# Operands normalised before their split, sums read from PSUM by ScalarE and by the convolution, weights in half blocks, and another order of the units

## The chip, the cores and the metric

The kernel runs on one core of a Trainium2 chip. Its metric is the device time of one execution in microseconds (us). Every number here is of float32 data; the large products are made of pieces that TensorE takes as `float32r`.

## The reference, cut to what matters

One inference step of a two-layer decoder trunk, for 512 prompt tokens and 8 sample tokens (520 columns in all) of 1024 features:

```python
xn = rmsnorm(x, g_mix)                       # over the 1024 features of a token
u_a, v_a, q, k, v, gate_a, gate_b = split(xn @ w_in)     # 512, 512, 3 x 768, 2 x 1024 columns
a_out = chunk_spatial_gate(gelu(u_a), rmsnorm(gelu(v_a), g_v), w_s, b_s)
q, k = rope(rmsnorm(q)), rope(rmsnorm(k))    # 12 heads of 64: three pairs (window, dilation)
b_out = windowed attention of each pair, the pairs merged by their softmax denominators
merged = sigmoid(gate_a) * (a_out @ w_a_proj) + sigmoid(gate_b) * (b_out @ w_b_proj)
x = x + merged @ w_o
up = rmsnorm(x, g_ffn) @ w_up                # 5632 columns
c = conv_b + sum(conv_w[j] * up shifted by 2 - j tokens for j in 0, 1, 2)
x = x + (silu(c_gate) * c_val) @ w_down      # 2816 inputs
```

Outputs are the new x of both token groups, new key and value rows, the last two up-projected rows and the samples' v rows.

## The kernel before, in words

Everything lies with features on the 128 partitions and the 520 tokens as columns. An output **unit** is 128 output features. Weights and activations are each split into a high part and a low part (what is left over), and a product is three matmuls: high x high, high x low, low x high. A matmul takes 128 inputs and 260 of the 520 columns, so a unit of eight input tiles is 48 matmuls, summed in an accumulator of two PSUM banks. `dense` (L263) issues a unit through `products` (L243, its matmul L252). `dense_first` (L383) does the first three units of layer 0 input by input, and `dense(xs, 2)` the first two of the other stages that follow a norm.

The weights of a unit are one load on SP's queue (`load_raw`, up to 512 KB) and one split (`split`, L187): ScalarE copies the high part (L193), VectorE subtracts (L194). Loads run three units ahead, splits two.

`Norm` does not normalise its operands: it splits x times the gain (L291, L292), sums the squares beside that, and a task (`rms`, lane "n") makes 1/rms per token, spread over all partitions. Every unit that reads such operands is multiplied by it as it leaves PSUM, on VectorE: L870 and L876 for q, k, v; L894 for u and v of the gate (`gelu2`, which goes on on GpSimd and ScalarE); L1051 for the gates, whose tanh follows on ScalarE (L1052); L1097 for the FFN. There `up_conv` then applies three taps to the copy in SBUF: one on ScalarE (L1100), two on VectorE (L1102).

The order of units in a layer is the list `units`: q, k, v of pair 2, four v units, pair 1, four u units, pair 0, then gate a and w_a in turn (eight of each), three gates b, then w_b and the other gates b in turn (b5, b6, b7 without a gate between them), eight units of w_o, and the FFN: 22 pairs of up units, the down work in three pieces of 8, 7 and 7 inputs, each eight units in a row after the first up pair of the next piece.

Attention, spatial gate, samples' attention, history and output rows are generators in lanes. `pump` weaves their stages between the matmuls by an estimate of time, `finish` forces lanes to their end. They use two PSUM banks for transposes (`tps`) and one score tile of two banks (`sc_tile`). The samples' attention multiplies cached values by weights on GpSimd (L834) and adds them on VectorE (L842, L844). From this program a planner that simulates the timeline makes each engine's fixed order; operations inside `urgent()` get a higher priority. Each engine then takes its instructions in that order.

## Time and profile before

| | |
|---|---|
| timed runs, median of 3 | 1584.09 us (1583.84 to 1584.78) |
| profiled execution, first to last instruction | 1582.3 us |
| TensorE busy | 1550.8 us (98%) |
| weight loads of TensorE busy | 1522.5 us (96%) |
| VectorE, ScalarE, GpSimd busy | 934.2, 648.2, 515.6 us |
| matmuls | 12985 recorded |

The span of the profiled execution is the only time that the page gives of it; it goes from the first to the last instruction, and the timed runs lie 1.8 us above it. A group of instructions is named by its line, engine, operation and tiles; "idle before" is what the engine waited in front of them, and the arrow names what released it. A window is a stretch of the span in us from its start. A few matmul records can be missing.

### The profile page before, as it was taken

The numbers are of one execution on the slowest core, as the hardware profiler recorded it, in microseconds if no ns is written. First come the engines' busy times: TensorE is split into PE (matmuls) and PEld (weight loads), VectorE is DVE, ScalarE is ACT, GpSimd is POOL, SyncE is SP. The second block draws the span as 40 slices with busy tenths as digits, with TensorE's granted clock in tenths as the row PEclk, the third lists the DMA queues.
The fourth block names the chain that finished last, engine by engine and source line by source line (L and its number), as shares of the span: only waits on it lengthen the run. The fifth ranks groups of instructions, "written<-read, shape, count | busy, mean of one in ns | idle before, by whom it ended". The sixth has DMA issues, their size and how long they took to land. (4 is left out here: it accounts for less than half of the span.)

```text
span 1582.3 us, 31439 instructions
## 1 busy us (share of the span) xinstructions
PE 1550.8 (98%) x12985; PEld 1522.5 (96%) x12985; DVE 934.2 (59%) x1344; ACT 648.2 (41%) x1155; POOL 515.6 (33%) x677
## 2 busy tenths in 40 slices
PE   8999999899999999999999999998999999999998
PEld 7989899899999999999999999998999999999998
DVE  6576856855466456556437585757655663564652
ACT  5454536334444234334435544552334441442342
POOL 3645453623222012213228272636222220220130
PEclk9999999999999999999999999999999999999999
DMA  7443333424233333332344332433332333323322
GB/s 211 132 115 112 95 107 102 152 78 131 84 94 94 94 94 86 88 95 85 108 113 126 111 125 79 120 113 113 99 115 82 93 94 94 94 84 104 92 73 70
DMA packets 294845, 164.24 MB, mean 104 GB/s; under 512 B 14143, under 2 KB 288335, under 8 KB 294687
## 3 DMA queue, kind: packets, MB, share of 16 engines
q1 hardware_dynamic: 294703, 162.24, 35.0%
q8 instruction: 102, 1.67, 0.4%
q14 instruction: 40, 0.33, 0.1%
HBM read 154.66 MB, written 10.36 MB: 104 GB/s over the span
## 5 line engine op out<-in xcount | busy, mean ns | idle before, releaser
L252 PE MATMUL acc<-t,whi 128*128 128x260 f32 x7776 | 1276.4, 285 | 11.1 <-DVE t L1051 8.7
L252 PEld LDWEIGHTS acc<-t,whi 128*128 128x128 f32 x7776 | 1070.7, 189 | 18.4 <-issue 11.6
L252 PE MATMUL acc<-t,wlo 128*128 128x260 f32 x3888 | 785.5, 284 | 0.0
L252 PEld LDWEIGHTS acc<-t,wlo 128*128 128x128 f32 x3888 | 600.4, 189 | 1.4 <-issue 0.7
L193 ACT CAST whi<-raw 128x1024 fp32r<-128x1024 f32 (+3 forms) x268 | 260.5, 973 | 457.4 <-PE acc L252 287.5
L194 DVE TENSOR_TENSOR wlo<-raw,whi 128x1024 fp32r<-128x1024 f32 (+3 forms) x268 | 323.0, 1206 | 40.3 <-ACT whi L193 22.9
L1097 DVE TENSOR_TENSOR t<-acc,t 128x520 f32<-128x520 f32 x88 | 61.5, 699 | 158.2 <-PE acc L252 158.2
L1098 POOL COPY ut<-t 128x10 f32<-128x10 f32 x88 | 30.9, 351 | 364.5 <-DVE t L1097 361.1
L1102 DVE SCALAR_TENSOR_TENSOR t<-t,cwc,t 128x511 f32<-128x511 f32 (+1 forms) x176 | 131.6, 749 | 4.9 <-ACT t L1100 1.8
L1131 DVE TENSOR_TENSOR x<-acc,x 128x520 f32<-128x520 f32 x48 | 33.5, 700 | 148.2 <-PE acc L252 148.2
L1124 POOL TENSOR_TENSOR t<-t,t 128x520 fp32r<-128x520 f32 x44 | 58.9, 1339 | 127.1 <-ACT t L1123 127.1
L300 POOL TENSOR_TENSOR t<-t,t 128x520 f32<-128x520 f32 x25 | 44.0, 1762 | 110.1 <-ACT t L299 107.5
L1100 ACT ACTIVATE t<-t,vcol,cwc 128x520 f32<-128x520 f32 x88 | 72.5, 824 | 5.8 <-DVE t L1097 5.5
L1123 ACT CAST t<-t 128x520 fp32r<-128x520 f32 x44 | 27.6, 627 | 115.2 <-DVE t L1121 115.2
L506 POOL TENSOR_TENSOR t<-t,t 128x128 f32<-128x128 f32 x96 | 56.7, 619 | 18.8 <-DVE ss L499 18.2
L1105 POOL TENSOR_TENSOR t<-t,hc 128x8 f32<-128x8 f32 x88 | 45.4, 515 | 49.7 <-ACT t L1100 49.7
L1120 ACT ACTIVATE t<-t 128x520 f32<-128x520 f32 x44 | 28.1, 639 | 81.1 <-DVE t L1102 81.1
L1075 POOL TENSOR_TENSOR t<-t,t 128x520 f32<-128x520 f32 x16 | 23.6, 1482 | 80.5 <-DVE t L1074 80.5
L653 ACT ACTIVATE t<-t,stat 128x128 f32<-128x128 f32 (+1 forms) x96 | 40.1, 420 | 22.9 <-DVE stat L650 22.7
L136 POOL TENSOR_TENSOR rr<-ss,mhalf 128x8 f32<-128x8 f32 (+1 forms) x30 | 49.0, 1632 | 0.0
L1051 DVE TENSOR_TENSOR t<-acc,t 128x520 f32<-128x520 f32 x32 | 22.2, 695 | 43.7 <-PE acc L252 43.7
L775 POOL TENSOR_TENSOR t<-t,t 128x512 f32<-128x512 f32 x24 | 35.1, 1473 | 30.3 <-DMA t<-in_cache_kv_w_dram 25.4
(195 smaller groups left out, 1172.2 us busy)
## 6 DMA issues: line engine op xcount, KB each, us to landing
raw<-in_w_up_dram SPq DMA_DIRECT2D x88, 512.0 KB
raw<-in_w_in_dram SPq DMA_DIRECT2D x84, 512.0 KB
raw<-in_w_down_dram SPq DMA_DIRECT2D x32, 448.0 KB
t<-in_cache_kv_w_dram SPq DMA_DIRECT2D x48, 256.0 KB
raw<-in_w_o_dram SPq DMA_DIRECT2D x16, 512.0 KB
raw<-in_w_down_dram SPq DMA_DIRECT2D x16, 512.0 KB
raw<-in_w_a_proj_dram SPq DMA_DIRECT2D x16, 256.0 KB
out_dram<-t SPq DMA_DIRECT2D x15, 256.0 KB
```

The source lines that it names most:

```text
L136: pool.tensor_tensor(out, in_, mhalf[: in_.shape[0], :n], op=ALU.pow)
L193: act.copy(hi[:, :nk], r)
L194: eng.tensor_tensor(lo[:, :nk], r, hi[:, :nk].bitcast(F32), op=ALU.subtract)
L252: mm = pe.matmul(acc[:, h, :H2], w[:, k], m[:, h * H2 : h * H2 + H2], start=(k == 0 and i == 0), stop=(k == last and i == 2),)
L300: eng.tensor_tensor(self.ssum[i], self.ssum[i], sq, op=ALU.add)
L506: pool.tensor_tensor(s4[:, i, :, s : s + 32], q4[:, i, :, d : d + 32], ts_[:n, i : i + 1, s : s + 32].to_broadcast([n, 4, 32]), op=ALU.mult,)
L653: act.activation(S[:, hp], S[:, hp], AF.Exp, bias=nmx[:, i : i + 1], accum_out=stat[:, 4 + i : 5 + i])
L1097: dve.tensor_tensor(v2(up), acc, rb, op=ALU.mult)
L1100: act.activation(cv, up, AF.Identity, scale=cwc[:, 2, i : i + 1], bias=vcol[:, 32 + i : 33 + i])
L1102: dve.scalar_tensor_tensor(cv[:, s:TP], up[:, : TP - s], cwc[:, j, i : i + 1], cv[:, s:TP], op0=ALU.mult, op1=ALU.add)
L1105: pool.tensor_tensor(cv[:, TP:], cv[:, TP:], hc[:, :, m], op=ALU.add)
L1124: pool.tensor_tensor(lo, cg, hi.bitcast(F32), op=ALU.subtract)
```

## The change

- Weights are loaded and split in blocks of at most four input tiles (half a unit), with a ring of six split blocks and nine raw ones.
- Accumulators are five single banks, transposes and scores share three banks; a score takes two of those three.
- `dense` takes any number of units at once and hands each one's two banks to a function `unit`, inside `urgent()`. The first two units after a norm, of w_o and of the last down piece (three in layer 0's start) are taken input by input.
- After 1/rms is there, a second task (`operands`, lane "x") multiplies x by gain and 1/rms and splits the product again; `dense2` uses these operands, so nothing has to be multiplied on the way out of PSUM. It serves pairs 1 and 0, u, v, all gates, and the up units from the fourth on (`NSTD = 3`).
- Their sums are read from PSUM by ScalarE (q, k, v, u, v: copies; gates: tanh), and in the FFN by the three taps (`psum_conv`).
- Gates come in pairs: g g, g g a a, g g a a, g g a a, a a; then for b the order `mix`. The down work is four pieces of 7, 5, 5 and 5 inputs, of which three are spread between later up pairs.
- `SEVEN` names unit pairs that would be computed as seven products of half operands; it is empty.

```diff
-NSLOT = 66
+NSLOT = 61
+RING = 6
+RAWS = 9
+NSTD = 3
+SEVEN = ()
...
     def acc_tile():
-        return ps.tile([128, 2, 512], F32, tag="acc", name=nm("acc"))
+        return ps.tile([128, 512], F32, tag="acc", bufs=5, name=nm("acc"))[:, :H2]
     def tps():
-        return ps.tile([128, 512], F32, tag="tp", name=nm("tp"))
+        return ps.tile([128, 512], F32, tag="tp", bufs=3, name=nm("tp"))
...
+    pieces = ((0, 7), (7, 12), (12, 17), (17, 22))
+    for i in range(22):
+        ffn.append(("up", i))
+        for g, i0, ns in ((0, 8, (2, 2, 2, 2)), (1, 13, (2, 2, 2, 2)), (2, 18, (1, 1, 2, 4))):
+            if 0 <= i - i0 < 4:
+                ffn.extend(("down", g, sum(ns[: i - i0]) + j) for j in range(ns[i - i0]))
+    mix = ("g0", "g1", "b0", "g2", "b1", "b2", "g3", "b3", "b4", "b5", "b6", "b7")
...
     def feed():
+        while st["split"] < len(blocks) and (st["split"] < RING or st["split"] - RING in st["used"]):
+            split()
+        while st["raw"] < len(loads) and st["raw"] < st["taken"] + RAWS - 4:
+            load_raw()
...
+    def dense(xs, unit, lows_last=False):
+        banks = [[acc_tile(), acc_tile() if j < 2 else tps()[:, :H2]] for j in range(len(cs))]
+        def taken(j):
+            finish("n")
+            with urgent():
+                unit(j, *banks[j])
+        for k0, k1 in ks:
+            for j, c in enumerate(cs):
+                held[j, k0] = block(g, (k0, c))
+            last = k1 == nk and not lows_last
+            for js in [[j] for j in range(len(cs))] if last else [range(len(cs))]:
+                for k in range(k0, k1):
+                    for j in js:
+                        hi, lo = held[j, k0]
+                        triple((hi[:, k - k0], lo[:, k - k0]), xs[k], banks[j], k == 0, k == nk - 1, ...)
+                if last:
+                    taken(js[0])
...
+    def dense2(norm, unit, done):
+        finish("n", "x")
+        if groups[st["g"]][0] == "u":
+            for j in range(2):
+                dense(norm.xn, lambda _, *accs, j=j: unit(j, *accs))
+            return
...
+        def operands(self):
+            while any(tasks["n"]):
+                yield -1.0
+            for s in range(7 if self.seven else 5):
+                with urgent():
+                    for m in (s, s + 4) if s < 4 else ():
+                        xm = tmp()
+                        dve.scalar_tensor_tensor(xm, x[:, m], vcol[...], self.rbc, op0=ALU.mult, op1=ALU.mult)
+                        high(m, xm)
+                    if 0 <= s - 1 < 4:
+                        for m, i in ((k, (1, 0)), (k + 4, (2, 3))):
+                            xn[m] = low(m)
+                yield -0.7
...
-            sc = sc_tile()
+            sc = [tps(), tps()]
...
+        def copied(g, accs):
+            for h, acc in enumerate(accs):
+                act.copy(v2(g)[:, h], acc)
...
-        def gate(g):
-            acc = dense(xs)
-            with urgent():
-                dve.tensor_tensor(v2(g), acc, rb, op=ALU.mult)
-            act.activation(g, g, AF.Tanh, scale=0.5)
+            def unit(j, *accs):
+                g[j] = tmp()
+                for h, acc in enumerate(accs):
+                    act.activation(v2(g[j])[:, h], acc, AF.Tanh, scale=0.5)
...
+        m1, gb, mgs = [], [], []
+        for j in range(5):
+            if j < 4:
+                m1.extend(gates())
+            if j == 1:
+                finish("v")
+            for i in (2 * j - 2, 2 * j - 1) if j else ():
+                gated(m1[i], As)
+        for g, j in mix:
+            if g == "g":
+                gb.extend(gates())
+                continue
+            if j == 0:
+                finish("a", "s")
+            gated(gb[j], Bx)
...
+        def psum_conv(m, z0, z1):
+            for h, z in enumerate((z0, z1)):
+                act.activation(v2(cv)[:, h], z, AF.Identity, scale=cwc[...], bias=vcol[...])
+            act.copy(ut[:, :, m], z1[:, 510 - H2 :])
+            for j, s in ((1, 1), (0, 2)):
+                for z, c0, c1 in ((z0, s, H2), (z0, H2, H2 + s), (z1, H2 + s, TP)):
+                    src = z[:, c0 - s : c1 - s] if z is z0 else z[:, c0 - s - H2 : c1 - s - H2]
+                    dve.scalar_tensor_tensor(cv[:, c0:c1], src, cwc[...], cv[:, c0:c1], op0=ALU.mult, op1=ALU.add)
```

## Rows read from the trace of the kernel before

**Rows 1.** The page's first section: busy time of each engine, share of the span, instructions.
```profile
PE 1550.8 (98%) x12985; PEld 1522.5 (96%) x12985; DVE 934.2 (59%) x1344; ACT 648.2 (41%) x1155; POOL 515.6 (33%) x677
```

**Rows 2.** Waits of TensorE over the span: waited for, us in total, times, longest us.
```profile
PE acc L252 <- DVE t L1051: 8.7, 4, 4.0
...
PE tp L368 <- DMA t<-in_x_prompt_dram: 3.0, 2, 1.8
PE sc L630 <- DVE t L644: 2.7, 5, 1.2
PE tp L612 <- DVE t L521: 2.6, 3, 1.5
PE acc L252 <- DVE t L1074: 2.3, 2, 1.2
```

**Rows 3.** Stretches: length, busy us (instructions) by engine, granted clock, DMA share, GB/s.
```profile
0.00:20.00 20.00, 12.97 (x77) 11.78 (x78) 11.71 (x20) 11.26 (x17) 4.41 (x7) 1.00 0.98 263
33.00:53.00 20.00, 20.00 (x168) 20.00 (x169) 8.11 (x10) 9.17 (x16) 4.75 (x3) 1.00 0.70 200
60.00:100.00 40.00, 35.70 (x300) 33.80 (x300) 32.79 (x54) 20.55 (x48) 32.70 (x36) 1.00 0.42 124
...
300.00:400.00 100.00, 94.28 (x773) 93.72 (x772) 61.97 (x76) 34.68 (x54) 31.20 (x26) 0.98 0.36 106
430.00:760.00 330.00, 330.00 (x2762) 330.00 (x2761) 187.20 (x225) 120.79 (x145) 65.03 (x106) 1.00 0.32 92
```

**Rows 4.** Groups by line and shape over the span: count, busy us, mean ns; idle before.
```profile
L194 DVE TENSOR_TENSOR wlo<-raw,whi 128x1024 fp32r<-128x1024 f32 x204 | 269.7, 1322 | 38.6 <-ACT whi L193 22.5 <-issue 1.3 <-PE acc L252 0.8
L193 ACT CAST whi<-raw 128x1024 fp32r<-128x1024 f32 x204 | 214.2, 1050 | 336.0 <-PE acc L252 209.2 <-issue 115.1 <-DMA raw<-in_w_in_dram 8.2
L1100 ACT ACTIVATE t<-t,vcol,cwc 128x520 f32<-128x520 f32 x88 | 72.5, 824 | 5.8 <-DVE t L1097 5.5
...
L1102 DVE SCALAR_TENSOR_TENSOR t<-t,cwc,t 128x511 f32<-128x511 f32 x88 | 65.8, 748 | 1.8 <-ACT t L1100 1.8
L1097 DVE TENSOR_TENSOR t<-acc,t 128x520 f32<-128x520 f32 x88 | 61.5, 699 | 158.2 <-PE acc L252 158.2
...
L292 DVE SCALAR_TENSOR_TENSOR t<-x,vcol,t 128x520 fp32r<-128x520 f32 x32 | 25.8, 817 | 0.0
...
L335 DVE TENSOR_TENSOR t<-t,t 128x520 fp32r<-128x520 f32 x24 | 17.4, 733 | 7.7 <-ACT t L334 7.7
...
L644 DVE TENSOR_TENSOR t<-sc,cst 128x256 f32<-128x256 f32 x36 | 13.5, 411 | 0.0
...
L194 DVE TENSOR_TENSOR wlo<-raw,whi 128x512 fp32r<-128x512 f32 x16 | 11.4, 715 | 0.5 <-ACT whi L193 0.5
...
L193 ACT CAST whi<-raw 128x512 fp32r<-128x512 f32 x16 | 9.9, 618 | 11.5 <-issue 9.6 <-PE acc L252 1.7
...
L581 ACT COPY t<-tp 128x256 f32<-128x256 f32 x24 | 8.9, 369 | 9.5 <-PE tp L580 9.3
```

**Rows 5.** Timeline of VectorE around the first long wait: start us, us, engine line.
```profile
300.44 2.54 DVE L842 TENSOR_TENSOR t<-t,t 128x512 f32<-128x512 f32 x2
303.08 1.09 DVE L844 TENSOR_TENSOR t<-t,t 128x256 f32<-128x256 f32 x1
304.09 0.69 DVE L1051 TENSOR_TENSOR t<-acc,t 128x520 f32<-128x520 f32 x1
```

**Rows 6.** Timeline of ScalarE in the same stretch, idle us before it in brackets.
```profile
304.81 0.64 ACT L1052 ACTIVATE t<-t 128x520 f32<-128x520 f32 x1 [5.90 <-DVE t L1051]
```

**Rows 7.** Timeline of VectorE in the run of b units of layer 0.
```profile
364.46 2.35 DVE L194 TENSOR_TENSOR wlo<-raw,whi 128x1024 fp32r<-128x1024 f32 x1 [0.20 <-ACT whi L193]
366.73 0.68 DVE L1074 SCALAR_TENSOR_TENSOR t<-t,acc 128x520 f32<-128x520 f32 x1
```

**Rows 8.** Timeline of VectorE: first and last evacuation of layer 0's first six units.
```profile
33.57 0.69 DVE L876 TENSOR_TENSOR t<-acc,t 128x520 f32<-128x520 f32 x1
...
52.44 0.70 DVE L876 TENSOR_TENSOR t<-acc,t 128x520 f32<-128x520 f32 x1 [3.65 <-PE acc L252]
```

More of the change, by code (lines that the diff above doesn't have):

```diff
@@ new lines, in step_kernel @@
+        for j in range(2, 8):
+            one(a["w_o"][l], 0, 8, j * 128)
+        for op, i, *m in ffn:
+            if op == "down":
+                k0, k1 = pieces[i]
+                one(a["w_down"][l], k0, k1 - k0, m[0] * 128)
+            elif i == 0:
+                one(a["w_up"][l], 0, 8, 0, DFF)
+            elif i < NSTD:
+                one(a["w_up"][l], 0, 8, i * 128)
+                one(a["w_up"][l], 0, 8, DFF + i * 128)
+            else:
+                two(("up", i), a["w_up"][l], DFF + i * 128, i * 128)
@@ L178, in urgent, with load_raw @@
+    raws, splits, parts4 = [], {}, {}
+    st = {"raw": 0, "taken": 0, "split": 0, "used": set(), "g": 0, "now": 0.0, "last": -9.0,
+          "pin": False}
+    at = {b: i for i, b in enumerate(blocks)}
     def urgent():
         return tc.high_priority(URGENT)
-    def load_raw(u):
-        w, k0, nk, c0 = units[u]
-        r = wp.tile([128, 8, 128], F32, tag="raw", bufs=4, name=nm("raw"))
+    def load_raw():
+        w, k0, nk, c0 = loads[st["raw"]]
+        st["raw"] += 1
+        r = wp.tile([128, 4, 128], F32, tag="raw", bufs=RAWS, name=nm("raw"))
@@ L184, in load_raw, with next_raw @@
         dma(r[:, :nk], w[k0 * 128 : (k0 + nk) * 128, c0 : c0 + 128].rearrange("(k p) m -> p k m", p=128))
[L185 to L191 removed]
+        raws.append(r[:, :nk])
+    def next_raw():
+        if not raws:
+            load_raw()
+        st["taken"] += 1
+        return raws.pop(0)
@@ L263, in dense, with triple @@
-    def dense(xs, n=1):
-        us = []
-        for _ in range(n):
-            feed()
-            us.append((*splits.pop(st["u"]), acc_tile()))
-            st["u"] += 1
-        nk = len(xs)
-        assert all(u[2] == nk for u in us)
-        for k in range(nk):
-            products(us, xs, k, (0, 1, 2), nk - 1)
-        accs = [u[3][:, :, :H2] for u in us]
-        return accs if n > 1 else accs[0]
+    def triple(w, x, bank, start, stop, which=(0, 1, 2)):
+        pump()
+        st["now"] += 0.12 * len(which) * len(bank)
+        for i in which:
+            wi, xi = ((w[0], x[0]), (w[0], x[1]), (w[1], x[0]))[i]
+            for h, b in enumerate(bank):
+                mm = pe.matmul(
+                    b,
+                    wi,
+                    xi[:, h * H2 : h * H2 + H2],
+                    start=start and i == 0,
+                    stop=stop and i == 2,
+                )
+                if st["pin"]:
+                    tc.keep_in_program_order(mm)
+                    st["pin"] = False
@@ new lines, in qkv_units @@
+            n = 3 if l == 0 else 2
+            first = [0]
+            def unit(j, *accs):
+                g = tmp()
+                normed(g, accs)
+                have(first[0] + j, g)
+            dense(xs, unit, l == 0)
+            if l == 0:
+                t = tps()
+                pe.transpose(t[:, :104], vrow[:104], ident[:104, :104])
+                act.copy(vcol[:, 16:], t[:, :104])
+            for i in range(n, 6):
+                first[0] = i
+                dense(xs, unit)
@@ L1054, in step_kernel, with gates, unit, done @@
-        m1 = []
-        for j in range(8):
-            g = tmp()
-            gate(g)
-            if j == 0:
-                finish("v")
-            acc = dense(As)
-            with urgent():
-                dve.scalar_tensor_tensor(v2(g), v2(g), 1.0, acc, op0=ALU.add, op1=ALU.mult)
-            m1.append(g)
-        add("v", history())
-        gb = [tmp() for _ in range(8)]
-        for j in range(NGB):
-            gate(gb[j])
-        finish("a", "s")
-        mgs = []
-        for j in range(8):
+        def gates():
+            g = {}
+            def unit(j, *accs):
+                g[j] = tmp()
+                for h, acc in enumerate(accs):
+                    act.activation(v2(g[j])[:, h], acc, AF.Tanh, scale=0.5)
+            def done(j, t):
+                g[j] = t
+                act.activation(t, t, AF.Tanh, scale=0.5)
+            dense2(norm, unit, done)
+            return [g[0], g[1]]
```

475 lines of the change are left out of this document (302 added, 173 removed).

## The prediction, made before the change was run

> **What bounds the kernel now.** I read the page's first section first: TensorE is busy 1550.8 of 1582.3 us [rows 1]. So at most 31.5 us of the span can be won without taking matmuls away, and no matmul is taken away: `SEVEN` is empty, so `dense2` always takes its first branch, two calls of `dense`, and a unit of eight inputs is still 8 x 3 x 2 = 48 matmuls of 260 columns. The seven-product code of the diff never runs. The table of stretches then says what a matmul costs: in the FFN 2762 fill 330.00 us without a gap, 0.1195 us each [rows 3]. A unit of eight inputs lasts 48 x 0.1195 = 5.7 us, one of four 2.9, of two 1.4; a down unit of seven inputs 5.0, of five 3.6.
>
> Where the 31.5 us lie is in the same table: 7.0 in the first 20 us, 4.3 in 60:100, 5.7 in 300:400, none in the FFN [rows 3]. The view of waits names them: 8.7 us for accumulators that a gate's evacuation (L1051) had not freed, four times, 4.0 at the longest; 2.3 for accumulators behind L1074, the b units' evacuation; 3.0 for the first inputs; 2.7 for the score tile; 2.6 for turned q and k [rows 2]. The second layer repeats the first.
>
> What the longest wait is made of is read from VectorE's timeline. The gate's evacuation starts at 304.09, because VectorE's queue is in order and holds the adds L842 and L844 of the samples' attention ahead of it: from 300.44 on they run one behind the other, 2.54 and 1.09 us [rows 5]. Meanwhile ScalarE stood idle for 5.90 us [rows 6].
>
> **The change part by part.** All terms are of the span of the profiled execution, 1582.3; the median of the timed runs, 1584.09, is 1.8 above it, and I add that 1.8 at the end.
>
> *Gates evacuated by ScalarE, in pairs.* The multiply by 1/rms (32 on VectorE, like the 0.699 of L1097) goes; Tanh is taken from the two PSUM banks, 2 x about 0.37 (the 256-column PSUM copy of L581) [rows 4]. In the two long stalls ScalarE was free [rows 6], so these evacuations no longer stand behind L842: of 8.7 us all could go. But the w_a evacuations stay on VectorE, and the new order puts four of them (a4 to a7) in a row just where the samples' adds run. A block of 4 us against a slack of one unit (2.9 us, since with five banks unit n+2 needs the first bank of unit n) leaves 1.1 us per layer. Bounds -8.7 and 0; I take -6.5.
>
> *b units.* Before, b5 to b7 run without a gate between them and cost 2.3 us in two layers: a weight split of 2.35 us stood ahead of an evacuation [rows 7]. Now five run in a row, 5 x 1.4 = 7.2 us, in which VectorE has 10 half evacuations of 0.41 (L644, 256 columns out of PSUM), five half splits of 0.715 and some of the L335 of 0.733 [rows 4]: 4.1 + 3.6 + 1.5 = 9.2 us of work. The backlog of 2.0 less a slack of 1.4 is 0.6 us by undisturbed durations; with the splits as slow as the row of 2.35 against 1.322 shows [rows 4, 7] it is 2 to 3. Bounds -2.3 (five banks absorb it) and +4; I take +1.5 for both layers.
>
> *Tokens normalised ahead.* Four norms get a second set of operands: 8 multiplies (0.817, as L292) and 8 subtracts (0.733, as L335) on VectorE, 12.4 us, and 8 copies on ScalarE of about 0.64, as a plain 520-column pass has it (5.1 us) [rows 4, 6]. In the FFN six units with the old operands (34 us) cover them, in layer 1 too. In layer 0 it is tight: 1/rms is there when the first evacuation starts, 33.57, and the sixth unit ends where its evacuation starts, 52.44 [rows 8]. In 33:53 VectorE has 8.1 us of work now [rows 3]; 12.4 more make 20.5 of 20, while the first unit on the new operands needs the fourth input only 2.2 us later and is taken input by input. Bounds 0 and +4 (12.4 of work against the 11.9 free, and a queue that is sometimes wrongly ordered); I take +0.5. There are 61 tile slots for 66, with 16 more tiles alive while both sets are; that can hold back stages beside the path, whose last date, `finish("a", "s")` ahead of b0, lies one gate (5.7 us) later than now: nothing.
>
> *First units input by input, weights in halves.* Each half is loaded and split by itself: ScalarE 2 x 0.618 for 1.050, VectorE 2 x 0.715 for 1.322 [rows 4], 0.2 and 0.1 us more per unit of 5.7, beside TensorE. The prefetch is no shorter (six half blocks split, five more loaded). Weight loads stand in SP's queue between the x loads at the start; half of each is 256 KB less three times, at 263 GB/s [rows 3] one microsecond each, and 3.0 us were waited for x there [rows 2]. VectorE limits what follows, so I take -1, bounds -2 and +1. The pairs at the start of w_o and of the last down piece win nothing: TensorE does not wait there now.
>
> *PSUM.* Before: two accumulators of two banks, one score tile of two, two for transposes. Now: five single accumulator banks and three for transposes and scores; a score takes two of these three. TensorE takes its instructions in order, so a transpose placed too early waits. Now the score tile costs 2.7 us in five waits; the longest sum of a transpose's waits, 2.6 us, is for its data, not for a bank [rows 2]. If score waits double and transposes wait 2.6 more, +5.3; if VectorE, relieved of the evacuations of q, k, v and of gelu (40 x 0.699 [rows 4]), is earlier with the scores, -2.7. I take +1.
> The Trainium skill (Perfetto Trace Analysis, Optimization Strategy) has a rule that speaks against this edit: the same gap repeating on the engine that should be saturated can mean that there is not enough SBUF or PSUM for the next tile. By it the score gaps should grow with the loss of a bank, +5.3 or more; by the rows alone, five waits among many scores, I stay at +1. It is the first rival below.
>
> *FFN.* Per up unit VectorE's 0.699 + 2 x 0.748 = 2.2 becomes four taps of 260 columns at 0.41 and two of one or two columns (at most 0.41, I take 0.2): 2.0. ScalarE's 0.824 becomes two halves of about 0.37 + 0.18 (the 0.18 is what L1100 with its scale and bias columns takes over a plain 520-column pass of 0.64) [rows 4, 6]. A unit's first bank is free 2 x 0.55 + 0.2 + 0.41 + 0.41 + 0.2 = 2.3 us after its last matmul, and is needed after one more unit: 5.7 us, or 3.6 where a down unit of five inputs follows. That holds with 1.3 us to spare, so 0; the cover gone (ScalarE and VectorE each behind another half split, +1.3) it would be some tenths at each of about 14 such places, +5. VectorE is at 187 of 330 us here [rows 3]. The down work in four pieces instead of three is 16 more evacuations in all, off the path.
>
> *Tail.* The last evacuation is two halves, 2 x 0.41 for 0.699: +0.1, nothing.
>
> Sum: -6.5 + 1.5 + 0.5 - 1 + 1 = -4.5. 1582.3 - 4.5 = 1577.8, and with the 1.8 a median of 1579.6 us.
>
> **The rivals.**
> 1. *Three banks are too few* (slower). In each attention block two of three banks are held until both masks are added; every transpose of the other three blocks in flight, of the merges and of the spatial gate goes through the third. For it: in 60:100 VectorE is at 32.8 and GpSimd at 32.7 of 40 us [rows 3], so banks are freed late. Against: only 2.7 us for 24 scores so far [rows 2]. If each of the 24 scores costs 0.6 us, about the mean of the five waits (2.7/5 = 0.54), that is 14 less the 2.7 there now: +11.3 in place of my +1, 1589.9. From 0.34 us a score on ((5.5 + 2.7) / 24) the gain is eaten up.
> 2. *The stall moves to the w_a units* (no change). The block of adds in VectorE's queue [rows 5] stays, and four short units in a row meet it with less slack than a gate of 5.7 us. Then the -6.5 is about -2 and the rest +2: 1584.1. Against it: a fifth bank.
> 3. *VectorE's relief reaches the attention too.* 72 evacuations of 0.7 us leave its queue (32 + 40). All of the gates' 8.7 goes and half of the waits on L521 and L644 (2.65 of 5.3 [rows 2]), the b run costs what it cost: -8.7 - 2.65 - 1 + 0.5 = -11.85, 1572.2. Against it: GpSimd, on which many of VectorE's attention steps wait, is not relieved of anything in 60:100.
>
> **How the numbers follow.** The forecast gets 0.53, the first rival 0.20, the second 0.15, the third 0.12. A measurement tells 0.2% (3.2 us) from nothing: faster is below 1580.9. The forecast's own range is 1575 to 1584, since its terms' bounds rarely add up; three quarters of it are faster, 0.40, a fifth no change. With the third rival, faster is 0.52; no change 0.11 + 0.13 = 0.24; slower 0.20 from the first rival and 0.04 from the edges, 0.24. The range of eight in ten runs from the third rival's time to the first's, 1572 to 1590.
>
> **What would show it.** Right: TensorE's busy time stays at 1550 to 1551 and the FFN's matmuls at 0.1195 us; no wait of an accumulator for a gate; about 1 us per layer of waits on the w_a evacuation; some waits behind L1074's successor in the run of five b units; at 52 us a gap under 2. Wrong: score and transpose waits beyond 8 us in all (the first rival), accumulators that wait for the conv in the FFN, a change of the matmul's pace, or a start that loses more than it wins.

## The result, and the profile of the changed kernel

The changed kernel takes 1622.91 us (median of 4 runs, 1620.63 to 1625.82) where the kernel before, beside it, took 1584.43: 1.0241 times the time, interval 1.0226 to 1.0255. The forecast was 1579.6 with a range up to 1590, so the sign was wrong too. The profiled execution spans 1618.5 us, 36.2 more than before.

The page's line of busy times, which answers to [rows 1] (engine, busy us, share, instructions):

```profile
PE 1565.9 (97%) x12985; PEld 1535.5 (95%) x12985; DVE 974.9 (60%) x1984; ACT 750.5 (46%) x1719; POOL 449.0 (28%) x601
```

TensorE executes the same 12985 matmuls, but is busy for 15.1 us more and idle for 52.6 instead of 31.5. The waits of TensorE, which answer to [rows 2] (waited for, us in total, times, longest):

```profile
PE acc L339 <- DVE t L1123: 12.2, 8, 2.3
PE acc L339 <- DVE t L1307: 11.7, 2, 6.0
PE acc L339 <- ACT t L1060: 4.9, 4, 1.4
...
PE tp L810 <- DVE t L719: 3.6, 3, 1.3
PE tp L476 <- POOL rc L137: 2.1, 1, 2.1
PE tp L1177 <- POOL t L1154: 2.0, 1, 2.0
PE tp L587 <- DMA t<-in_x_prompt_dram: 2.0, 3, 0.7
PE tp L866 <- ACT t L868: 1.7, 2, 1.5
PE tp L828 <- ACT t L813: 1.6, 2, 0.8
```

An evacuation is the instruction that reads a finished sum out of its accumulator and so frees the bank. L1123 is that of the units that still use the old operands (`normed`, VectorE), L1307 the one of w_a (`gated`, VectorE), L1060 the copy of q, k, v (ScalarE). No line is a gate's tanh. The stretches of [rows 3] (length; busy us by engine in the order PE, PEld, DVE, ACT, POOL; granted clock; DMA share; GB/s), and three more, of the stall at w_a, layer 0's first up units and layer 1's start:

```profile
0.00:20.00 20.00, 13.98 (x85) 12.53 (x86) 12.28 (x21) 8.91 (x15) 5.76 (x10) 1.00 0.80 217
33.00:53.00 20.00, 16.31 (x118) 14.85 (x118) 15.95 (x27) 9.81 (x18) 5.33 (x4) 0.91 0.46 125
60.00:100.00 40.00, 37.72 (x306) 35.90 (x306) 31.43 (x55) 24.01 (x59) 29.47 (x35) 1.00 0.43 124
300.00:400.00 100.00, 93.87 (x766) 93.46 (x765) 58.65 (x95) 34.72 (x73) 30.35 (x26) 0.97 0.33 97
312.00:318.00 6.00, 4.03 (x18) 4.03 (x19) 5.82 (x12) 0.00 (x0) 0.26 (x1) 0.50 0.31 91
427.00:468.00 41.00, 37.24 (x307) 36.59 (x307) 30.39 (x54) 21.51 (x35) 9.10 (x13) 1.00 0.28 79
800.00:900.00 100.00, 94.72 (x741) 92.12 (x740) 66.25 (x117) 57.44 (x125) 42.51 (x45) 0.95 0.42 118
```

33:53 holds 118 matmuls for 168 before. From 312 to 318 the clock stands at 0.50, its lower level, 1.2 GHz. The trace's clock records show such stretches of 3.4 us or twice that six times before the tail, 27 us in all (at 38.7, 311.7, 830.6, 840.8, 885.2 and 1107.0 us, each during or shortly after a stall of TensorE); the kernel before has two, 6.8 us in all. 18 matmuls take 4.03 us there, where 18 of 0.1195 us are 2.15. If a matmul takes twice as long in all of these stretches, they cost up to half their length, 13.6 us against 3.4; in 4.5 of the 27 us TensorE stood anyway, which leaves some 8 us more than before. That is about half of the 15.1 us by which TensorE's busy time rose with the same work. Of the rest 3 us lie in layer 0's first stage; what makes them was not looked into.

Where the 36 us lie is worked out by marking the stages off by their counts of 260-column matmuls (a stage lasts from the previous stage's last matmul to its own; us, before and after):

```
                                     layer 0           layer 1
pair 2 of q, k, v (288)              52.1   61.1       36.5   44.7
v (192)                              29.0   31.3       29.1   32.1
pair 1, u, pair 0 (768)             128.0  128.2      127.2  127.9
gates, w_a, gates, w_b (1056)       157.0  160.1      156.2  159.0
w_o (384)                            47.5   46.4       47.4   46.3
up units 0 to 2 (288)                36.4   40.7       36.3   42.3
rest of the FFN (2880)              345.4  344.2      347.5  348.2
```

Three places lose: the start of each layer (11.3 and 11.2 us), the first up units (4.3 and 6.0), and gates, w_a and b, where I had seen a gain (3.1 and 2.8).

What a start of an FFN looks like is read from VectorE's timeline (start us, us, engine, line):

```profile
445.39 1.43 DVE L520 SCALAR_TENSOR_TENSOR t<-x,vcol,t 128x520 f32<-128x520 f32 x2
446.73 0.75 DVE L1364 SCALAR_TENSOR_TENSOR t<-t,cwc,t 128x511 f32<-128x511 f32 x1
447.39 1.31 DVE L506 TENSOR_TENSOR t<-t,t 128x520 fp32r<-128x520 f32 x2
448.61 0.76 DVE L520 SCALAR_TENSOR_TENSOR t<-x,vcol,t 128x520 f32<-128x520 f32 x1
449.28 0.69 DVE L278 TENSOR_TENSOR wlo<-raw,whi 128x512 fp32r<-128x512 f32 x1
449.88 0.75 DVE L1364 SCALAR_TENSOR_TENSOR t<-t,cwc,t 128x510 f32<-128x510 f32 x1
450.55 0.69 DVE L278 TENSOR_TENSOR wlo<-raw,whi 128x512 fp32r<-128x512 f32 x1
451.15 0.76 DVE L520 SCALAR_TENSOR_TENSOR t<-x,vcol,t 128x520 f32<-128x520 f32 x1
451.82 1.31 DVE L506 TENSOR_TENSOR t<-t,t 128x520 fp32r<-128x520 f32 x2
453.04 0.76 DVE L1123 TENSOR_TENSOR t<-acc,t 128x260 f32<-128x260 f32 x2
```

L520 and L506 make the normalised operands. From 445.39 to 453.04 not one accumulator is emptied. TensorE, which has five banks for units of two, goes on for one unit and then stands:

```profile
453.52 0.50 PE L339 MATMUL acc<-t,whi 128*128 128x260 f32 x2 [2.30 <-DVE t L1123]
```

The stall at w_a, on VectorE and on TensorE, and in the third fence GpSimd at the start of layer 0 and (its last line) beside the stall:

```profile
306.18 2.98 DVE L1040 TENSOR_TENSOR t<-t,t 128x512 f32<-128x512 f32 x2
309.25 1.09 DVE L1042 TENSOR_TENSOR t<-t,t 128x256 f32<-128x256 f32 x1
310.26 1.52 DVE L278 TENSOR_TENSOR wlo<-raw,whi 128x512 fp32r<-128x512 f32 x1
311.71 1.88 DVE L1040 TENSOR_TENSOR t<-t,t 128x512 f32<-128x512 f32 x2
313.50 0.42 DVE L1307 SCALAR_TENSOR_TENSOR t<-t,acc 128x260 f32<-128x260 f32 x1
```
```profile
307.66 0.28 PE L339 MATMUL acc<-t,whi 128*128 128x260 f32 x1
313.98 1.02 PE L339 MATMUL acc<-t,whi 128*128 128x260 f32 x3 [6.03 <-DVE t L1307]
```
```profile
32.62 2.63 POOL L1154 TENSOR_TENSOR t<-t,cst 128x512 f32<-128x512 f32 x2 [1.92 <-DMA t<-in_w_s_dram]
35.24 1.92 POOL L1159 TENSOR_SCALAR t<-t 128x512 f32<-128x512 f32 x1
37.13 1.20 POOL L137 TENSOR_TENSOR rc<-ms,mhalf 128x5 f32<-128x5 f32 x1
...
305.67 5.57 POOL L1032 TENSOR_TENSOR t<-t,sc 128x512 f32<-128x512 f32 x4
```

L1040 and L1042 are the samples' adds, the same block that [rows 5] shows ahead of a gate. L137 is the power that makes 1/rms; its input was there at 33.4, but GpSimd first waits for w_s and masks it. The diff has moved layer 0's first units behind `add("v", a_branch(), 12.0)` and `add("s", attn_samples(), 12.0)`: in planned time the two side tasks start 17 us earlier than they did (11 us in layer 1).

### The profile page after: what moved, and what is told of

It reads as the page before. It is cut to its first block, busy times and chain, and to the rows that moved or that the text cites. A ratio compares the mean times of both kernels' runs of the same rounds, so it can differ in the third digit from the quotient of the medians.

```text
span 1618.5 us, 33598 instructions
## 1 busy us (share of the span) xinstructions
PE 1565.9 (97%) x12985; PEld 1535.5 (95%) x12985; DVE 974.9 (60%) x1984; ACT 750.5 (46%) x1719; POOL 449.0 (28%) x601
## 5 line engine op out<-in xcount | busy, mean ns | idle before, releaser
L339 PE MATMUL acc<-t,whi 128*128 128x260 f32 x7792 | 1313.5, 285 | 30.7 <-DVE t L1123 12.2
L339 PEld LDWEIGHTS acc<-t,whi 128*128 128x128 f32 x7792 | 1101.8, 190 | 39.6 <-DVE t L1123 14.1
L339 PE MATMUL acc<-t,wlo 128*128 128x260 f32 x3896 | 847.6, 285 | 0.0
L278 DVE TENSOR_TENSOR wlo<-raw,whi 128x512 fp32r<-128x512 f32 (+2 forms) x536 | 378.8, 707 | 465.6 <-ACT whi L277 396.4
L277 ACT CAST whi<-raw 128x512 fp32r<-128x512 f32 (+2 forms) x536 | 311.3, 582 | 637.8 <-PE acc L339 547.5
L1387 DVE SCALAR_TENSOR_TENSOR t<-acc,cwc,t 128x259 f32<-128x259 f32 (+2 forms) x456 | 146.1, 386 | 1.3 <-ACT t L1375 0.6
L1390 POOL TENSOR_TENSOR t<-t,hc 128x8 f32<-128x8 f32 x76 | 15.6, 205 | 380.9 <-ACT ut L1382 380.9
L1375 ACT ACTIVATE t<-acc,vcol,cwc 128x260 f32<-128x260 f32 x152 | 77.6, 560 | 0.0
L1339 DVE TENSOR_TENSOR x<-acc,x 128x260 f32<-128x260 f32 x128 | 48.7, 422 | 27.2 <-PE acc L339 26.8
L137 POOL TENSOR_TENSOR rr<-ss,mhalf 128x8 f32<-128x8 f32 (+1 forms) x30 | 50.0, 1668 | 0.0
L1032 POOL TENSOR_TENSOR t<-t,sc 128x512 f32<-128x512 f32 x24 | 31.0, 1308 | 2.9 <-ACT t L926 2.5
```

Of the source, the lines that this page charges most:

```text
L137: pool.tensor_tensor(out, in_, mhalf[: in_.shape[0], :n], op=ALU.pow)
L277: act.copy(hi[:, :nk], r)
L278: eng.tensor_tensor(lo[:, :nk], r, hi[:, :nk].bitcast(F32), op=ALU.subtract)
L339: mm = pe.matmul(b, wi, xi[:, h * H2 : h * H2 + H2], start=start and i == 0, stop=stop and i == 2,)
L1339: dve.tensor_tensor(xm, acc, xm, op=ALU.add)
L1375: act.activation(v2(cv)[:, h], z, AF.Identity, scale=cwc[:, 2, i : i + 1], bias=vcol[:, 32 + i : 33 + i],)
```

## The experiments

All times are medians, in brackets the ratio to runs of the kernel before (1583.8 to 1585.4) on the same chip and its 95% interval. Lengths of stages, waits and the clock are those of each run's one profiled execution. Where a run's lines are numbered otherwise, the text says which line it is.

**1. Without the priority of the operands.** Theory: they stand ahead of the evacuations because they are urgent.

```diff
             for s in range(7 if self.seven else 5):
-                with urgent():
+                if True:
```

> The changed kernel, with the second set of operands made without the higher priority, so that the planner puts evacuations and weight splits ahead of it on VectorE and ScalarE; nothing else differs. Theory A (the second set, made in a burst ahead of the evacuations, costs the time: against the kernel before, the stretches of the first six units, of v and of the first six up units are longer by 9.0, 2.4, 4.3 us in layer 0 and 8.2, 2.9, 6.0 in layer 1): the waits of accumulators for L1123 (12.2 us) go almost, and 15 to 25 us with the clock that they cost: 1598 to 1608. Rival B (too few PSUM banks for transposes and scores): no change, 1623. Rival C (the work of the second set itself, whatever its place in the queue): the first unit on the new operands waits instead, 1615 to 1623.

1626.67 us (1.0256, 1.0234 to 1.0278). The order of every engine came out the same as with the priority; the operands keep their place by the time at which the planner issues them. The lever didn't move the thing, so this run says nothing on the theory. It is the changed kernel measured once more, and tells how far such measurements lie apart: 1620.76 to 1628.08 us for 1620.63 to 1625.82, and in the profiled execution 41.0 us at half level for 27 and 63.9 us in layer 0's first stage for 61.1. Differences of up to 4 us between the runs below, or of up to 3 us in a stage, show little by themselves.

**2. One set of operands.** No second set: VectorE scales by 1/rms at every evacuation, and the FFN's sums go through that multiply before the taps, as in the kernel before. All else of the change stays.

```diff
-            add("x", self.operands(), delay + 0.1)
...
-                dense(norm.xn, lambda _, *accs, j=j: unit(j, *accs))
+                        dve.tensor_tensor(v2(t)[:, h], acc, norm.rb[:, h], op=ALU.mult)
+                dense(norm.xs, scaled)
```

> The changed kernel without the second set: all units take the first operands, and VectorE multiplies by 1/rms on the way out of PSUM, as before the change; order of units, banks and half blocks stay as changed. Theory A: the excess of the six stretches above goes but for what the start of layer 0 has (about 6 us): 1623 - 33 + 6 = 1596, give or take 6. Rival B: 1620 to 1628, the same kernel with VectorE busier. Rival C says as A.

1595.16 us (1.0064, 1.0048 to 1.0081), 28 less than the changed kernel and 31.5 less than run 1, beside which it ran, with the first up units at 36.4 and 36.3 us again and pair 2 of layer 1 at 37.3. In the stretch that covers layer 0's first up units TensorE has no gap, although VectorE's evacuations are back:

```profile
427.00:468.00 41.00, 41.00 (x344) 40.76 (x343) 27.23 (x49) 19.58 (x30) 10.09 (x18) 1.00 0.32 91
```

The stages where the operands are made or first used (pair 2, v, first up units) together are 25.6 us shorter, of 27.7 between the two profiled executions. So the second set, with the evacuations that go with it, is most of the loss. Pair 2 of layer 0 still takes 59.5 us. TensorE still stalls at w_a (5.0 us at the longest), but the evacuation that it waits for there is the one of a gate, which VectorE has again.

**3. Gates and w_a in turn, as before.** Is the stall at w_a made by four w_a units in a row?

```diff
-        for j in range(5):
-            if j < 4:
-                m1.extend(gates())
...
+        for j in range(8):
+            dense(norm.xn, tanh)
+            gated(m1[j], As)
```

> The changed kernel with gates a and w_a in turn, one of each, as before the change, instead of g g, then g g a a and so on. Theory D (four short w_a units in a row, whose evacuations stand on VectorE behind the samples' adds, cost two waits of 6.0 us and 6.8 us at the half clock after each): 12 + 6.8 us go, some of it comes back at single w_a units: 1604 to 1612. Rival: the block of adds in VectorE's queue stops the next accumulator whatever the order, as in the kernel before with 4.0 us a layer: 1617 to 1623. Theory A says nothing on this run.

1626.92 us (1.0269, 1.0251 to 1.0286): no gain, against run 1 beside it neither. The waits show a shorter stall at the same evacuation (L1305 here):

```profile
PE acc L337 <- DVE t L1305: 8.0, 2, 4.1
```

and the clock records show 10.2 us at half level with each instead of 6.8. The block of adds hits whichever evacuation of VectorE comes next, as it did a gate before.

**4. Two half blocks at a time at the start.** Are late second halves of the weights what slows the start of layer 0?

```diff
         if k in (1, 3, 5):
             load_raw()
+            load_raw()
...
         if k in (1, 3, 5):
             split()
+            split()
```

> The changed kernel with two half blocks loaded and split at each of the three places at the start where it does one, so that the first three units' weights come as early as in the kernel before. Theory E (the second halves come late, ScalarE's queue waits for them, and 1/rms of layer 0 is done at 39.9 us against 33.5): the stretch of the first six units loses 5 to 7 of its 9.0 us: 1616 to 1618. Rival (VectorE's work on the eight features sets it): 1 us at most, 1622.

1626.94 us (1.0264, 1.0248 to 1.0279), the stage 63.8 us. The power of 1/rms came at 39.09, still behind the masks, which now waited 3.22 us for w_s. The second halves did come earlier (the sixth split began at 17.0 us for 22.3), and the stage was no shorter. The theory fell as far as this run can tell: with 1/rms behind the masks it can't show what the half blocks cost alone.

**5. The side tasks as late as before.**

```diff
-        add("v", a_branch(), 12.0)
-        add("s", attn_samples(), 12.0)
+        add("v", a_branch(), 29.0 if l == 0 else 23.0)
+        add("s", attn_samples(), 29.0 if l == 0 else 23.0)
```

> The changed kernel with the mixer's two side tasks (a_branch with its masks of w_s on GpSimd, attn_samples) planned 17 us later in layer 0 and 11 us later in layer 1, where they stood before the change. Theory: in layer 0 GpSimd's mask multiplies (2.63 x2 + 1.92 us, first waiting 1.92 us for w_s to land) stand ahead of the power that makes 1/rms, so the first evacuations and, behind them, TensorE wait. Then the power runs near 33 instead of 37.1 us, the q/k/v units of pair 2 of layer 0 take 54 to 57 instead of 61.1 us, in layer 1 some 2 to 4 us go too, and the time falls by 6 to 10 us, to 1613 to 1619. Rival: the evacuations are late because the normalised operands are queued ahead of them on VectorE; then the power is earlier, the stage stays at 60 to 62 us and the time within 2 us of 1623.

1619.78 us (1.022, 1.0206 to 1.0234), 3 us less, half of the least that I expected, with intervals that overlap. GpSimd now makes 1/rms on time, and VectorE shows what took over (one fence each):

```profile
32.60 1.21 POOL L137 TENSOR_TENSOR rc<-ms,mhalf 128x5 f32<-128x5 f32 x1 [1.30 <-DVE ms L470]
```
```profile
36.47 0.75 DVE L520 SCALAR_TENSOR_TENSOR t<-x,vcol,t 128x520 f32<-128x520 f32 x1
37.13 0.68 DVE L278 TENSOR_TENSOR wlo<-raw,whi 128x512 fp32r<-128x512 f32 x1
37.74 2.09 DVE L520 SCALAR_TENSOR_TENSOR t<-x,vcol,t 128x520 f32<-128x520 f32 x3
39.75 1.30 DVE L506 TENSOR_TENSOR t<-t,t 128x520 fp32r<-128x520 f32 x2
40.97 0.75 DVE L1123 TENSOR_TENSOR t<-acc,t 128x260 f32<-128x260 f32 x2
```

1/rms was 4.5 us earlier, the first evacuation 1.1 (40.97 for 42.03): the operands, due as soon as 1/rms is there, stand ahead of it. The rival held for layer 0, with 60.9 us for the stage. v (2.0 us) and layer 1's start (4.4) became shorter, but pair 1, u and pair 0 of layer 1 took 131.2 us for 127.9, and the whole profiled execution is as long as without the edit (1618.7, 1618.5). A gain of this edit by itself is not shown.

**6. The operands' steps 4.4 us apart.** This does move them: one or two evacuations stand between any two steps.

```diff
-                yield -0.7
+                yield -4.0
             self.xn = [xn[m] for m in range(8)]
```

> The changed kernel with the steps that make the normalised operands planned 4.4 us apart instead of 0.8, so that one or two evacuations stand between any two of them on VectorE in both FFNs and in layer 1. Theory: what costs is that four to eight of VectorE's 1.3 to 1.4 us instructions per step stand in one block ahead of an evacuation, not their sum. Then the first up units go from 40.7 and 42.3 to 36.5 to 38 us, pair 2 of layer 1 from 44.7 to 37 to 39.5 us, the half clock after them goes, and the time falls by 11 to 17 us, to 1606 to 1612. Rival 1: VectorE has no room at all for the operands in these stages (their sum counts, wherever they stand): less than 4 us. Rival 2: the operands are then late for the first unit that uses them, TensorE waits there for the highs or lows, and the time stays within 4 us of 1623 or rises.

1609.59 us (1.0164, 1.0149 to 1.018), 13.3 less with the same instructions. Pair 2 of layer 1 went from 44.7 to 37.3 us, its first up units from 42.3 to 39.1; those of layer 0 stayed at 40.7. The waits for L1123 halve:

```profile
PE acc L339 <- DVE t L1123: 5.9, 3, 2.4
```

That the block, and not only the sum, costs is shown for about half of the second set's 28 us.

**7. Late tasks and spread operands together.**

> The changed kernel with late side tasks and the operands' steps 4.4 us apart together. Theory of two causes in layer 0's first stage: with late tasks alone the power was early but the operands stood ahead of the evacuations, with spread operands alone the power was late; each alone left the stage at 60 to 61 us, both together bring it to 54 to 57 us, and the time to 1601 to 1606 (the spread run has 1609.6). Rival: the first stage waits for something else (the second half blocks' landing, the multiplies beside the lows): it stays at 59 us or more, and the time at 1606 to 1612.

1616.13 us (1.0198, 1.0182 to 1.0213), 6.5 more than run 6, with ranges that lie apart. The first stage is 58.4 us, better than either alone, but v takes 33.0 (29.8 in run 6), and the FFN of layer 0 349.6 us (344.9), where TensorE now waits for the operands' lows:

```profile
PE acc L339 <- DVE t L506: 2.6, 2, 1.8
```

The two causes don't simply add; the second rival of run 6 (operands too late for their first user) shows here.

**8. Spread operands, their lows on GpSimd.** Half of the second set's work leaves VectorE.

```diff
-                dve.tensor_tensor(lo, src, hi.bitcast(F32), op=ALU.subtract)
+                pool.tensor_tensor(lo, src, hi.bitcast(F32), op=ALU.subtract)
                 return hi, lo
```

> The changed kernel with operands 4.4 us apart (1609.6 us) and the eight subtracts that make their lows (L506, 1.3 us for two on VectorE) on GpSimd. Theory: what is left of the second set's cost is VectorE's sum of work in the stages where it makes them (up 0 to 2: 40.7 and 39.1 instead of 36.4 and 36.3; pair 2 of layer 0 60.2 instead of 52 to 55 us); with half of it gone up 0 to 2 take 37 to 38.5 us, layer 0's first stage 57 to 59, and the time is 1601 to 1606. Rival 1: the wait is for the multiplies, which stay: 1608 to 1611. Rival 2: GpSimd's subtracts are late or slow VectorE's instructions beside them (its add took 1.27 us beside GpSimd and 0.68 us alone): over 1611, with waits of TensorE for lows.

1606.99 us (1.0143, 1.0129 to 1.0157), 2.6 below run 6, with overlapping runs. The first up units fell to 37.7 and 37.8 us, as the sum of work would have it, though a block without the lows is also shorter; the first stage of layer 0 rose to 63.3, where GpSimd has the late power too. What remains of the second set at the layers' starts isn't settled by this.

**9. One set, late tasks.** Run 2 with the edit of run 5.

> One set of operands (no normalised copies; VectorE scales by 1/rms at the evacuation, as in the run with one set, 1595.2 us) and the two side tasks planned late. Theory: the 7.4 us that pair 2 of layer 0 still lost with one set are the wait for 1/rms behind the masks of w_s. Then that stage takes 52 to 54.5 instead of 59.5 us and the time is 1586 to 1590, 0.1 to 0.4% over the kernel before. Rival: the wait comes from the evacuation by two instructions with one bank each or from late half blocks of weights: the time stays at 1593 to 1597.

1592.62 us (1.0048, 1.0036 to 1.0061), 2.5 below run 2, with overlapping runs. Without the operands, 1/rms on time does reach the stage: 55.1 us for 59.5. Part of it came back: v takes 30.5 us for 28.5, and layer 1 is 2.3 us longer, with 3.4 us at half clock at 972.5.

**10. The same, the samples' sum in steps 2.2 us apart.**

```diff
-                yield -0.7
+                yield -2.0
                 p, c, cv = got.pop(0)
```

> As the run with one set and late side tasks, and the steps of the samples' weighted sum of cached values (a multiply on GpSimd and an add on VectorE each) planned 2.2 us apart instead of 0.8. Theory: the stall of some 4 to 6 us of TensorE near the first w_a units comes from those adds standing in a block on VectorE, each waiting for GpSimd, ahead of one evacuation, and costs its length and the half clock behind it (3.4 or 6.8 us at half level). Then both stalls and the half clock near 306 and 1084 us are gone and the time is 8 to 14 us below that of the run without the spread, 1574 to 1580, faster than the kernel before. Rival: spread adds still wait for GpSimd one by one, and each holds an evacuation (many waits of about 1 us), or the samples' result comes too late for the first b units: within 3 us of that run.

1592.47 us (1.005, 1.0038 to 1.0063): nothing. The stalls are shorter and more (the longest 3.3 us for 4.9, still behind a gate's evacuation). Issued 2.2 us apart, the steps still run together, since GpSimd's multiplies wait for the cache's transfers; VectorE's adds (L1046) then stand in twos ahead of an evacuation (L1313, the w_a of this kernel):

```profile
308.46 2.30 DVE L1046 TENSOR_TENSOR t<-t,t 128x512 f32<-128x512 f32 x2 [0.94 <-POOL t L1038]
310.68 0.75 DVE L1313 SCALAR_TENSOR_TENSOR t<-t,acc 128x260 f32<-128x260 f32 x2
```
```profile
307.21 2.23 POOL L1038 TENSOR_TENSOR t<-t,sc 128x512 f32<-128x512 f32 x2 [1.41 <-DMA t<-in_cache_kv_w_dram]
```

**11. The kernel before, the samples' adds on GpSimd.**

```diff
-                    dve.tensor_tensor(av, av, cv, op=ALU.add)
+                    pool.tensor_tensor(av, av, cv, op=ALU.add)
```

> The kernel before with one thing changed: the adds of the samples' weighted sum of cached values (L842, L844; 12 to 14 per layer) on GpSimd instead of VectorE. Theory: from 285 to 313 us VectorE has no idle time (the add takes 0.68 us alone and 1.27 us beside GpSimd's multiplies), so the evacuations of the last gates and of w_a stand behind a block of adds; without them the 4.0 us stall, the 3.4 us at half clock behind it, and their twins in layer 1 go: 6 to 12 us less, 1573 to 1579. Rival: GpSimd now needs multiply and add in turn (some 1.1 to 1.5 us each) and the result is late: TensorE waits for the samples' part at the first b units, or the attention's multiplies on GpSimd stand behind the adds: 1582 to 1592.

1587.66 us (1.0018, 1.001 to 1.0027), the rival. The stall at the gates went (no gap in gates and w_a in either layer), but the sum came late, and TensorE waits at its product (L850):

```profile
PE tp L850 <- DVE t L846: 8.9, 2, 7.5
```

**12. The changed kernel with late tasks, spread operands and the adds on GpSimd** (run 7 with the edit of run 11).

> As the run with late tasks and spread operands, and the adds of the samples' sum on GpSimd. Theory: the two stalls of 5.9 us at the first w_a unit and 6.8 us at half clock behind each go; w_a, b and gates of a layer take 150 to 153 instead of 160 us; 10 to 17 us less than the run without it, 1587 to 1594, so that what the changed kernel loses is accounted for by operands in a block, 1/rms behind the masks, and the adds, and the rest is within 10 us of the kernel before. Rival: the evacuations of w_a are held by other work of VectorE (the attention's tails, low halves of weights): 4 us less or nothing.

1603.91 us (1.0114, 1.0098 to 1.0129), 12.2 below run 7, but above the 1587 to 1594 that I expected: the three causes don't account for the kernel with the second set. 19 us over the kernel before are left, with 59.0 us in layer 0's first stage, 40.7 in the first up units of either layer and 32 in v, and the samples' sum comes late (TensorE waits 3.5 us for it). No wait for L1307 is left; gates, w_a and b take 154.0 and 152.5 us for 159.6 and 158.8. VectorE empties the first w_a unit as it comes, and TensorE is full in the stretch that held the stall (one fence each):

```profile
308.00 0.75 DVE L1307 SCALAR_TENSOR_TENSOR t<-t,acc 128x260 f32<-128x260 f32 x2
310.02 0.75 DVE L1307 SCALAR_TENSOR_TENSOR t<-t,acc 128x260 f32<-128x260 f32 x2
```
```profile
307.00:319.00 12.00, 12.00 (x102) 12.00 (x101) 9.40 (x15) 2.81 (x5) 11.84 (x11) 1.00 0.32 91
```

**13. One set, late tasks, adds on GpSimd** (run 9 with the edit of run 11).

> One set of operands, late side tasks, and the adds of the samples' sum on GpSimd (against the same without the last, 1592.6 us). Theory: the stalls of 4.9 us at w_a and 6.8 us at half clock behind them in each layer go, and the order of the gates and b units, which gives the sum some 10 us more room than before, hides its later end: gates, w_a and b of a layer take 152 to 154.5 instead of 158 us; 8 to 12 us less, 1580 to 1585. Rival: the VectorE work that is left (scaled gates and w_a in one place) still holds the evacuations: 1588 to 1592.

1582.36 us (0.9983, 0.9974 to 0.9992): 10.3 below run 9, and 0.17% below the kernel before. Gates, w_a and b: 152.4 us in both layers, no half clock before the tail.

**14 and 15. The kernel before, adds on GpSimd, `NGB = 4`, then 5**: more gates ahead of the first b unit.

> The kernel before with the adds of the samples' sum on GpSimd and four gates of the other branch instead of three ahead of the first b unit (5.6 us more until the sum is needed). Theory: with the adds on GpSimd alone the w_a stall went (gates and w_a 90.9 and 91.1 us without an idle TensorE) but the sum came 7.5 us late in layer 1 (10.2 us at half clock behind it) and 1 to 2 us late in layer 0; with 5.6 us more room that wait falls to 0 to 2 us: 1574 to 1580, faster than the kernel before (1585). Rival: GpSimd has the adds one behind the other up to 323 and 1102 us and its later work shifts with them, or one more gate makes its own queue of evacuations: 1583 to 1589.

> The kernel before with the adds of the samples' sum on GpSimd and five gates of the other branch ahead of the first b unit (5.6 us more room than with four). Theory: the waits for the sum (2.2 and 2.9 us) and the 6.8 us at half clock go, b units with their gates take 60 to 61.5 us in both layers instead of 61.4 and 65.3: 1574 to 1578. Rival: five gates in a row hold up the evacuations or the low halves of the weights there, or the stage's end was not the sum's: 1580 to 1584.

1581.3 us (0.9979, 0.997 to 0.9988) and 1581.31 (0.9987, 0.9978 to 0.9996). Both are faster than the kernel before, by 0.1 to 0.2%, but less so than I expected, and the second gate more gave nothing. TensorE's timeline shows why: L850 waits as long at the same time with five gates (these rows) as with four:

```profile
322.96 0.61 PE L850 MATMUL tp<-cst,t 128*128 128x8 f32 x4 [2.14 <-DVE t L846]
1100.06 0.68 PE L850 MATMUL tp<-cst,t 128*128 128x8 f32 x4 [2.86 <-DVE t L846]
```

(324.39 and 1100.98, 2.16 and 2.93 with four.) With five, L850 stands some 7 us ahead of the first b unit: the product of the sum is issued where the planner takes it to be due, not where that unit needs it, so the room did not reach it.

Run 14 is also what run 13 has to be held against, since both have the adds on GpSimd: 1581.3 and 1582.4 us, with ranges that overlap. With the second set and the early tasks gone, what is left of the change (banks, half blocks, the order of the units) is worth nothing that these runs show.

## Why the prediction was wrong

**The step that failed is "Tokens normalised ahead", +0.5 us with bounds 0 and +4.** Measured by run 2 it is about 28 us (with the evacuations that run 2 moves back to VectorE). The instructions are as long as I took them (L520 0.754 us for 0.817, L506 0.728 for 0.733). What failed is "In the FFN six units with the old operands (34 us) cover them, in layer 1 too": it sets a sum of work against a sum of time. An engine that works in order has to be asked another question: how long does the next evacuation stand behind what is queued before it, against how long TensorE can go on without it. That was 7.6 us of one queue (445.39 to 453.04) against one unit of 5.7. Run 6, the same work in other places, shows it for 13 of the 28 us; in run 8, with half of that work off VectorE, the first up units fell further (40.7 and 39.1 us to 37.7 and 37.8), be it by the smaller sum or by shorter blocks. The rest, most of it in layer 0's first stages and around v, wasn't taken apart further.

**Uncounted: the clock after a stall.** [rows 3] held the sign, 0.98 for the stretch with the long stall, and I priced every stall at its length. The half-level stretches add up to 27 us for 6.8: by the estimate above some 8 us of the 36.

**Uncounted: a moved step.** With the first units taken into `qkv_units(2)`, the side tasks start earlier, and GpSimd's masks stand ahead of 1/rms, 3.7 us late (37.13 for 33.4). In the kernel with one set undoing it shortens layer 0's first stage by 4.4 us (run 9); in the total runs 5 and 9 gave 3 and 2.5 us, no more than repeated measurements lie apart, and run 7 lost 6.5. What the step is worth in the total stays open.

**Gates evacuated by ScalarE, -6.5: wrong.** The gates' waits did go, but the stall moved to w_a, my second rival, and at a higher price: stalls of 6.0 and 5.7 us, each with 6.8 us at half clock, where my term had 1.1 us per layer from a block of 4 us. The block was longer, because it held more: from 306.18 to 313.50 four adds of 512 columns, the short one and a split of weights, where [rows 5] has two adds and the short one. An add took 1.06 us on the mean (L1040, 22 of them in 23.3 us), about as before the change (L842, 1.04); with GpSimd idle it takes 0.69. With the adds off VectorE, gates, w_a and b take 154.0 and 152.5 us with tanh from PSUM on ScalarE (run 12) and 152.4 with VectorE's multiply (run 13): what [rows 2] showed as a wait for the gates' evacuation was the price of the adds, and the engine of the gates made no gain that these runs show.

**b units, +1.5: too dear.** TensorE has no gap there in the run of five; the lower bound's "five banks absorb it" was right.

**First units and half blocks, -1.** The first 20 us carry 13.98 us of matmuls for 12.97, as forecast; most of what was lost behind went to the two steps above. But run 9, free of both, still has 55.1 us for 52.1: +3.0 and outside my bounds. No run parts the half blocks from the rest here, so the cause of these 3 us stays open.

**PSUM, +1: right in size.** Pairs 1 and 0 and u together cost 0.2 and 0.7 us more. TensorE waits 7.6 us in front of the attention's transposes and scores (L810, L866, L828), and 9.6 with the transposes of w_s (L1177), which wait for GpSimd's masks and not for a bank. Before the change the same kinds of wait came to 8.0 us, so the 8 us that I had set as the mark of the first rival is where they already stood, and tells nothing. The Trainium skill (Perfetto Trace Analysis, Optimization Strategy) has the rule that the same gap repeating may mean too little PSUM for the next tile. By it these waits should have grown by 5 us or more; the trace doesn't agree. Run 13, with the same three banks, loses nothing in these stages but 1.5 us in layer 1.

**FFN, 0, and tail: right.** The rest of the FFN changed by -1.2 and +0.7 us, with no wait of an accumulator for the conv.

**What adds up.** Runs 2, 9 and 13 take away the second set, the early side tasks and the adds one after another: 1595.2, 1592.6 and 1582.4 us for 1622.9. So the loss is found, but the adds cost the kernel before as well (run 14), and the second set's part is only half taken apart.

## What to carry to other kernels

Price work that is moved onto an engine by the queue ahead of the next instruction that TensorE depends on, not by the engine's free time in the stage; and ask of each new task when it becomes due, since "as soon as its input is there" puts all of it in one block. A stall is priced with the clock behind it, and where a block of one kind of work causes a stall, taking the waiting instruction elsewhere only lets the block hit the next one: move the block. When a task is issued earlier or later, look at every queue it passes, and at what it had stood behind.

## What the runs showed of the hardware

Stretches at half clock came with stalls of 4 to 6 us, but also behind single waits of 1.3 to 2.0 us (ending at 830.5, 840.1 and 884.0 us in the changed kernel), while waits of 2.3 us (ending at 453.5 and 1248.5) had none. They came in lengths of 3.4, 6.8 or 10.2 us; a stall that run 3 made shorter (4.1 us for 6.0) had a longer one (10.2 for 6.8), so a stall's price did not follow its length. Nor is it fixed for a program: run 1, with the same order on every engine, had 41.0 us at half level where the changed kernel had 27. And VectorE's add of 512 columns took 0.69 us while GpSimd did nothing (at 313.84) and 1.49 us, twice in a row, beside GpSimd's four multiplies of 1.39 us from 305.67: work given to GpSimd lengthens VectorE's queue too. The Trainium skill (SBUF — State Buffer, SBUF: two separate sides) states that a VectorE instruction with two SBUF inputs and a GpSimd instruction that reads SBUF exclude each other for their whole length. The rows agree in part. In the 5.57 us of the four multiplies VectorE also ran two adds, the short one (L1042) and parts of two splits; by the shortest lengths that they have (1.04 for a multiply, at 287.6 beside VectorE's products out of PSUM; 0.69 and 0.43 for the adds with GpSimd idle) the multiplies and adds alone are 5.97 us of work in turn. So both sides are slowed, but some of their recorded lengths still overlapped.
